# Between two layers: three projections begun early instead of two, row differences on VectorE, operands in the order of use

## The chip, the cores and the metric

The kernel runs on one core of one Trainium2 chip. The metric is the device time of one execution in microseconds (us). A core has five engines that this text names by the profile's letters: PE (TensorE, with PEld for its weight loads), DVE (VectorE), ACT (ScalarE), POOL (GpSimd) and SP (SyncE, which issues all transfers here; SPq is its DMA queue).

## The reference, cut to what matters

Two layers over x of 1024 tokens by 1024 features: a gMLP layer, then a dilated attention layer, each between two RMS norms and with a residual.

```python
for i in range(2):
    h = rms_norm(x, norm_pre[i])
    y = gmlp_mixer(h, ...) if i == 0 else dilated_attention_mixer(h, b_w_in, b_w_out, cos, sin)
    x = x + rms_norm(y, norm_post[i])

def dilated_attention_mixer(h, w_in, w_out, cos, sin):
    proj = h @ w_in                  # 1024 x 10240
    # 3 groups (window, dilation) = (128,1), (512,4), (2048,16); 16 heads of 64
    for g, (window, dilation) in enumerate(DILATED_GROUPS):
        q, k = rope(q_g), rope(k_g)
        o_g, lse_g = dilated_window_attention(q, k, v_g, window, dilation)
    alpha = softmax over g of lse_g
    return (sum_g alpha_g * o_g) * silu(z) @ w_out
```

## The kernel before, in words

**Products.** Every projection of the attention layer (layer B) is a chunk of 256 output columns for all 1024 tokens, computed as seven products instead of eight: rows and features of h are each halved (a11, a12 for tokens 0 to 511, a21, a22 for 512 to 1023), and sums and differences of the quarters are multiplied. A product is four times three matmuls of 128x128 by 128x512 (`mm3`, lines 82 to 85: each operand is split into a high and a low part), so 12 matmuls. A chunk is named by its columns: bv00, bv01, ... for values (quarter of the heads q, group g), bqk0_0_0, bqk0_0_1, ... for queries and keys (q, g, pair), bz for the gate. Below, a, b and c are the first three chunks bv00, bqk0_0_0 and bqk0_0_1, and a5 is product 5 of chunk a. Products 1 and 2 need the rows of tokens 0 to 511 alone (`put_top`), products 3 to 7 need all rows (`put_rest`): the sum a21+a22 for product 5, three differences, one after the other in place, for 7 (a11-a21), 6 (sum minus a11) and 3 (a12 minus that), and a22 for 4. `put_op` brings each of them into the operand layout: four transposes on PE (line 129, tiles pt_b), a cast on ACT (b_hi), a subtraction on DVE (b_lo). Each is done per token tile of 128, as four calls of `put_rest`, the last two (b2 and b3) for the tiles 6 and 7.

**The weights.** `Right.load` fetches four pieces of 256 KB of a chunk (lines 169 to 171, tiles wb0 to wb3), `Right.sums` forms four sums on POOL (tiles wt1, wt2, wb1, wt4), and `get` splits an operand on ACT and DVE (whi, wlo). `Right.only` fetches just the one piece that product 1 or 2 needs, and no sums. Chunk.run stores product 1 in the bank pb, 2 in pa, 5 and 3 in pc; after 2 an add on DVE reads pa, after 7 an add reads pc (for a value chunk it is `vt <- p, b_x`, line 88), and product 3 goes on in pc and must wait for that add. The banks of PSUM are three of the kind "mm", and "s", "t", "o" for the attention's own tiles (2, 2 and 1).

**The transition.** The gMLP layer's output product (`wout_unit`) ends with the tiles 6 and 7; `post` then does, for one tile after the other, the post norm (ms_pa and rstd_pa, xr), the pre norm of layer B (ms_b, rstd_b, yt) and `put_rest`. The rstd of both norms is a 128x1 power on POOL (line 106). The first four tasks of layer B (products a1, a2, b1, b2) come from `run(pipeline(tasks[:4], 3, tasks[4:]))`, and here the scheduler places instructions on PE; from the fifth task on PE goes by the order of the program (`manual_schedule`). On the other engines the scheduler sets the order throughout.

**The rest.** `drive` runs the products and, between them, steps of the attention (`step_side`: four transposes pT or more, products po, scores s of one block; lines 766 to 820), which are queued with `later`; the attention of a query and key chunk is queued when its product 3 is done, with a wait of WAIT=16 yields (a yield is three matmuls, a quarter of a product). A credit that grows by RATE=0.125 a yield, from 0.5, lets one step through at each whole: one in two products. The rotated queries and keys are stored by SP into the tiles Q and K (lines 706 and 707, 16 transfers a chunk, eight after each half).

Of the kernel before, what the change touches and what calls it, by code (L numbers as in the profile page):

```python
# [23 lines left out]
RATE = 0.125  # L24
# [10 lines left out]
def trunk_kernel(  # L35
# [97 lines left out]
        put_op(ops, 1, h0[:, 0:512], t, name)  # L133
        put_op(ops, 2, h0[:, 512:1024], t, name)

    def put_rest(pool, ops, h0, h1, t, name, first):

        a11, a12, a21, a22 = h0[:, 0:512], h0[:, 512:1024], h1[:, 0:512], h1[:, 512:1024]
        s1 = pool.tile([P, 512], F32, tag="sums", bufs=2, name=f"sums_{name}")
        add(s1, a21, a22)  # L140
        sub(a21, a11, a21, first)
        sub(a11, s1, a11, nc.gpsimd)
        sub(a12, a12, a11, nc.gpsimd)
        for i, a in ((4, a22), (5, s1), (7, a21), (6, a11), (3, a12)):
            put_op(ops, i, a, t, name)

    HALVES = (slice(0, 512), slice(512, 1024))

# [130 lines left out]
    def in_turn(chunks, early=False, banks=5):  # L279

        out, n = [], 0
        if early:
            a, b = chunks[:2]
            out = [(a, 1), (a, 2), (b, 1), (b, 2), (a, 6), (a, 5), (a, 7), (b, 6), (a, 4)]
            out += [(a, 3), (b, 5), (b, 7)] if banks == 3 else [(b, 5), (a, 3), (b, 7)]
            n = 2
        for c, last in zip(chunks[n:], [chunks[n - 1] if n else None, *chunks[n:]]):
            if banks == 3:  # L290
                out += [(c, 1), (last, 4), (last, 3), (c, 6), (c, 2), (c, 5), (c, 7)]
            else:
                out += [(c, 1), (last, 4), (c, 2), (last, 3), (c, 6), (c, 5), (c, 7)]
        out += [(chunks[-1], 4), (chunks[-1], 3)]
        return [(c, i) for c, i in out if c]
# [240 lines left out]
    with ExitStack() as octx:  # L536
# [39 lines left out]
        def post(t):  # L576
            r = rstd_of(op, sq2[t], f"pa_{t}")
            xt = op.tile([P, D], F32, tag="wk", bufs=WK, name=f"xr_{t}")
            nc.sync.dma_start(out=xt, in_=x[t * P:(t + 1) * P, :])
            for hs_ in HALVES:  # L580
                nc.vector.scalar_tensor_tensor(out=xt[:, hs_], in0=yts[t][:, hs_], scalar=r, in1=xt[:, hs_], op0=ALU.mult, op1=ALU.add)
            nc.sync.dma_start(out=x1d[t * P:(t + 1) * P, :], in_=xt)
            norm_rows(op, yts[t], xt, g1b, f"b{t}")
            hs[t] = yts[t]
            if t < 4:
                put_top(bops, hs[t], t, f"b{t}")
            else:
                put_rest(op, bops, hs[t - 4], hs[t], t - 4, f"b{t - 4}", nc.vector)

        wout_unit((0, 1, 4, 5), 0)  # L590
        wout_unit((0, 1, 4, 5), 1)
# [69 lines left out]
    def v_chunk(q, g):  # L661
        vts = {}

        def out(th, ct):
            if ct not in vts:
                vts[ct] = qk_tile(f"vt_{q}_{g}_{ct}")
            return vts[ct][:, th * 512:th * 512 + 512]

        def turned(pr):
            V = v_tile(f"V_{q}_{g}_{pr}").rearrange("p (b h d) -> p b h d", b=8, h=2)  # L670
            for b4 in range(2):
                pt = psum("t", [P, 4, P], f"pvt_{q}_{g}_{pr}_{b4}")
                for j in range(4):
                    nc.tensor.transpose(out=pt[:, j, :], in_=toks(vts[pr], g, 4 * b4 + j, 1), identity=ident)
                nc.scalar.copy(out=V[:, 4 * b4:4 * b4 + 4].rearrange("p j h d -> p j (h d)"), in_=pt)
            VS[q, g, pr] = V
            yield

        def done():
            TURN[q, g] = turned(1)  # L680
            later(turned(0), 4)

        return proj_t(wb[q * 10 + g * 3], bops, newb, f"bv{q}{g}", lambda th, ct, o: None, out=out, done=done)

    def qk_chunk(q, g, pr):
        nm = f"{q}_{g}_{pr}"
# [20 lines left out]
                nc.sync.dma_start(out=half_of(dst[o + 32:o + 64, :], g, th), in_=by_block(yc[32 * i:32 * i + 32, :], g))  # L707

        def done():
            later(lambda: attention(q, g, pr), WAIT)  # L710
            if (q, g, pr) == (3, 2, 1):
                rate[0] = RATE3

        return proj_t(wb[q * 10 + g * 3 + 1 + pr], bops, newb, f"bqk{nm}", qk_out, done=done)

    def z_chunk(q):

        def z_out(th, ct, c):
            o = newb(f"z10_{q}") if (th, ct) == (1, 0) else c
            nc.scalar.activation(out=o, in_=c, func=AF.Silu)  # L720
            if q == 3:
                SZ[q, th, ct] = o
                return
            while (q, ct, th) not in merged:
                step_slow()
            y, kept = newb(f"y_{q}_{ct}_{th}"), ybd[2 * q + ct][:, HALVES[th]]
            nc.sync.dma_start(out=y, in_=kept)
            mul(o, o, y, nc.gpsimd)
            nc.sync.dma_start(out=kept, in_=o)

        return proj_t(wb[q * 10 + 9], bops, newb, f"bz{q}", z_out, hooks={2: lambda: prep(0), 7: lambda: prep(1)} if q == 3 else None)

    merged, through = set(), set()
    slow = deque()
# [216 lines left out]
            yield  # L951

    side = deque()
    credit, rate = [0.5], [RATE]
    now = [0]

    def later(work, wait=0):
# [68 lines left out]
                chunks.append(z_chunk(q - 1))  # L1026
    chunks += [z_chunk(2), z_chunk(3)]
    tasks = in_turn(chunks, True, 3)
    run(pipeline(tasks[:4], 3, tasks[4:]))
    with tc.manual_schedule(engines={mybir.EngineType.PE}):  # L1030
        drive(pipeline(tasks[4:], 3))


    for c in (6, 7):
# [141 lines left out]
```

## Time and profile before

| | |
|---|---|
| runs | 1915.05, 1915.68, 1916.51 us, median 1915.68 us |
| profiled execution | 1915.24 us, span 1913.5 us (1.74 us lie around it) |
| mean granted clock of TensorE over the span | 0.987 of full speed |
| busy: PE, DVE, ACT, POOL | 1834.7, 1310.4, 1002.7, 503.6 us |
| DMA | 242.22 MB, mean 127 GB/s |

A row of a timeline gives the start and the duration of one instruction or of a group of equal ones (x4), and in square brackets how long the engine had idled before it and for whom. Matmuls are pipelined: one lasts 0.39 us in the rows, and the next starts 0.23 us later. PEclk is the granted clock of TensorE as a share of 2.4 GHz: 1.00 is this level, 0.50 is 1.2 GHz, and a value between is a stretch with both.

### The profile page before, as it was taken

Reading aid. Unit: us, or ns where it says so; the run is one execution under the profiler, and the core shown is the slowest. Engines: PE = TensorE matmul, PEld = TensorE weight load, DVE = VectorE, ACT = ScalarE, POOL = GpSimd, SP = SyncE. Lnnn points to the kernel's source line nnn. Section 1 sums busy time; section 2 is a strip of 40 time slices with the busy share of each in tenths; the row PEclk is TensorE's granted clock in tenths of the full one; section 3 lists DMA queues with packets and bytes.
Section 4 is the critical chain, followed back from the end, with each engine's and each line's share of the span. In section 5 each row is a group of like instructions: output and inputs, shape, how many; then the busy total and the mean of one; then the engine's idle time right before and its main releaser. Section 6 shows DMA issues by size and latency. Waiting matters only on the chain.

```text
span 1913.5 us, 29729 instructions
## 1 busy us (share of the span) xinstructions
PE 1834.7 (96%) x10024; PEld 1507.0 (79%) x10024; DVE 1310.4 (68%) x2518; ACT 1002.7 (52%) x2280; POOL 503.6 (26%) x371
## 2 busy tenths in 40 slices
PE   6899999999999997999999999999999999999998
PEld 6899888888888775777788777788777787778777
DVE  7765766577455877558587695768684876868583
ACT  6544456555544664355555557364556445555831
POOL 3431343433300204222222113321233231221320
PEclk9999999999999998999999999999999999999999
DMA  6232434433256575232233544335533336423863
GB/s 214 86 125 93 139 116 129 128 111 101 78 193 231 171 252 171 69 81 73 81 81 92 165 129 128 75 78 132 163 102 97 82 89 163 133 75 84 248 196 110
DMA packets 231847, 242.22 MB, mean 127 GB/s; under 512 B 98448, under 2 KB 150288, under 8 KB 231696
## 3 DMA queue, kind: packets, MB, share of 16 engines
q1 hardware_dynamic: 231696, 240.34, 43.5%
q8 instruction: 79, 1.29, 0.3%
q14 instruction: 72, 0.59, 0.1%
HBM read 170.46 MB, written 44.63 MB: 112 GB/s over the span
## 4 chain that ended last, share of the span: by engine, by line
PE 72%; DVE 10%; DMA 5%; issue 3%; SPq 2%; ACT 2%; POOL 1%; DVEq 0%; POOLq 0%; ACTq 0%
PE p_bqk L83 6%; PE p_bqk L84 6%; PE p_bqk L85 6%; PE p_bv L83 4%; PE p_bv L85 3%; PE p_bv L84 3%; PE s L766 3%; PE po L815 3%; PE p_z L83 3%; PE p_z L84 2%; PE p_z L85 2%; PE pT L799 2%; PE p_u L83 2%; PE p_u L84 2%; PE po L84 2%
## 5 line engine op out<-in xcount | busy, mean ns | idle before, releaser
L83 PE MATMUL p_bqk<-b_hi,whi_bqk 128*128 128x512 f32 x672 | 270.2, 402 | 1.0 <-ACT b_x_bqk L240 0.9
L84 PE MATMUL p_bqk<-b_lo,whi_bqk 128*128 128x512 f32 x672 | 263.3, 392 | 0.0
L85 PE MATMUL p_bqk<-b_hi,wlo_bqk 128*128 128x512 f32 x672 | 263.3, 392 | 0.0
L777 ACT ACTIVATE St<-St,st 128x128 f32<-128x128 f32 (+1 forms) x384 | 168.5, 440 | 153.0 <-DVE st L774 150.9
L83 PEld LDWEIGHTS p_bqk<-b_hi,whi_bqk 128*128 128x128 f32 x672 | 127.0, 189 | 41.3 <-issue 10.5
L83 PE MATMUL p_bv<-b_hi,whi_bv 128*128 128x512 f32 x336 | 137.7, 410 | 12.2 <-DVE vt L88 11.1
L85 PEld LDWEIGHTS p_bqk<-b_hi,wlo_bqk 128*128 128x128 f32 x672 | 126.8, 189 | 27.2
L84 PEld LDWEIGHTS p_bqk<-b_lo,whi_bqk 128*128 128x128 f32 x672 | 127.1, 189 | 24.4
L85 PE MATMUL p_bv<-b_hi,wlo_bv 128*128 128x512 f32 x336 | 134.4, 400 | 0.0
L84 PE MATMUL p_bv<-b_lo,whi_bv 128*128 128x512 f32 x336 | 134.0, 399 | 0.0
L774 DVE CUSTOM_DVE_ANT_0 St<-s,mask 128x128 f32<-128x128 f32 (+1 forms) x384 | 110.6, 347 | 31.5 <-PE s L766 31.5
L84 PE MATMUL p_v<-wlo_v,a_hi 128*128 128x256 f32 x448 | 127.6, 285 | 3.9 <-DVE wlo_v L91 3.9
L85 PE MATMUL p_v<-whi_v,a_lo 128*128 128x256 f32 x448 | 127.8, 286 | 3.7 <-DVE sqa L368 2.2
L83 PE MATMUL p_v<-whi_v,a_hi 128*128 128x256 f32 x448 | 127.9, 286 | 2.9 <-DVE v_s_v L88 2.2
L91 POOL TENSOR_TENSOR wt_bqk<-wb_bqk,wt_bqk 128x512 f32<-128x512 f32 x48 | 71.3, 1485 | 194.6 <-DMA wb_bqk<-in_wb_dram 147.2
L91 DVE TENSOR_TENSOR wlo_bqk<-wb_bqk,whi_bqk 128x512 fp32r<-128x512 f32 x96 | 80.8, 842 | 54.0 <-ACT whi_bqk L97 53.4
L97 ACT CAST whi_bqk<-wb_bqk 128x512 fp32r<-128x512 f32 x96 | 59.4, 619 | 107.1 <-PE p_bqk L84 70.8
L85 PE MATMUL po<-oh,yl 128*128 128x512 f32 x256 | 101.6, 403 | 3.1 <-DVE yl L91 3.1
L83 PE MATMUL po<-oh,yh 128*128 128x512 f32 x256 | 101.9, 399 | 0.6 <-ACT yh L97 0.6
L84 PE MATMUL po<-ol,yh 128*128 128x512 f32 x256 | 100.9, 397 | 1.2 <-DVE ol L91 1.2
L91 POOL TENSOR_TENSOR wt_bqk<-wb_bqk,wb_bqk 128x512 f32<-128x512 f32 x24 | 33.7, 1405 | 246.9 <-DMA wb_bqk<-in_wb_dram 172.2
L766 PE MATMUL s<-K,Q 64*128 64x128 f32 (+1 forms) x768 | 85.8, 342 | 8.5 <-DMA K<-b_c 7.5
(262 smaller groups left out, 4843.5 us busy)
## 6 DMA issues: line engine op xcount, KB each, us to landing
wb_bqk<-in_wb_dram SPq DMA_DIRECT2D x96, 256.0 KB, 3.5
wr<-in_woa_dram SPq DMA_DIRECT2D x80, 256.0 KB, 3.5
yr<-yad SPq DMA_DIRECT2D x48, 256.0 KB, 3.3
wb_bv<-in_wb_dram SPq DMA_DIRECT2D x48, 256.0 KB, 3.2
Q<-b_c SPq DMA_DIRECT2D x192, 64.0 KB, 2.1
K<-b_c SPq DMA_DIRECT2D x192, 64.0 KB, 2.1
mo<-od SPq DMA_DIRECT2D x36, 256.0 KB, 3.5
mw<-wd SPq DMA_DIRECT2D x72, 128.0 KB, 3.5
```

The lines of the kernel that those rows point to most:

```text
L83: nc.tensor.matmul(out=pso, lhsT=l_hi, rhs=r_hi, start=start, stop=False, skip_group_check=chained)
L84: nc.tensor.matmul(out=pso, lhsT=l_hi, rhs=r_lo, start=False, stop=False, skip_group_check=chained)
L85: nc.tensor.matmul(out=pso, lhsT=l_lo, rhs=r_hi, start=False, stop=stop, skip_group_check=chained)
L91: (eng or nc.vector).tensor_tensor(out=out, in0=a, in1=b, op=ALU.subtract)
L97: nc.scalar.copy(out=hi, in_=src)
L766: nc.tensor.matmul(out=pss[hh][:, cs].rearrange("p (n l) -> p n l", l=k_.shape[2]), lhsT=q_, rhs=k_, start=True, stop=True)
L774: nc.vector.tensor_tensor_reduce(out=self.S[hh][:, cs], in0=pss[hh][:, cs], in1=mk, scale=-0.125, scalar=3.0e38, op0=ALU.add, op1=ALU.min, ...
L777: nc.scalar.activation(out=self.S[hh][:, cs], in_=self.S[hh][:, cs], func=AF.Exp, scale=-1.0, bias=m, accum_out=z)
L799: nc.tensor.transpose(out=pT[hh][:, k, :], in_=self.S[hh][:, k * P:k * P + P], identity=ident)
L815: nc.tensor.matmul(out=po[64 * hh:64 * hh + 64, o:o + m * P], lhsT=V[:, kb, hh, :], rhs=self.PT[:, hh, k:k + m, :].rearrange("p k i -> p ( ...
```

## The change

`put_rest` does the second difference on DVE too (only the third stays on POOL) and calls `put_op` in the order 5, 6, 7, 4, 3. `in_turn` begins with a1 a2 b1 b2 c1 c2, and the products 3 to 7 follow. Six tasks instead of four run ahead of `drive`, in a loop of their own, in which only the six weight pieces that they need are fetched; the full loads and sums of a, b and c come with the tasks after them. The bank of product 2 of a, b and c, and pc of a, is the single "o" bank (`EARLY_TAGS`). The first attention's wait is 12 yields instead of 16, and the credit starts at 0.

```diff
-    def put_rest(pool, ops, h0, h1, t, name, first):
+    def put_rest(pool, ops, h0, h1, t, name):
...
         add(s1, a21, a22)
-        sub(a21, a11, a21, first)
-        sub(a11, s1, a11, nc.gpsimd)
+        put_op(ops, 5, s1, t, name)
+        sub(a21, a11, a21)
+        sub(a11, s1, a11)
+        for i, a in ((6, a11), (7, a21), (4, a22)):
+            put_op(ops, i, a, t, name)
         sub(a12, a12, a11, nc.gpsimd)
-        for i, a in ((4, a22), (5, s1), (7, a21), (6, a11), (3, a12)):
-            put_op(ops, i, a, t, name)
+        put_op(ops, 3, a12, t, name)
...
-            a, b = chunks[:2]
-            out = [(a, 1), (a, 2), (b, 1), (b, 2), (a, 6), (a, 5), (a, 7), (b, 6), (a, 4)]
-            out += [(a, 3), (b, 5), (b, 7)] if banks == 3 else [(b, 5), (a, 3), (b, 7)]
-            n = 2
+            a, b, c = chunks[:3]
+            out = [(d, i) for d in (a, b, c) for i in (1, 2)]
+            out += [(a, 5), (a, 6), (a, 7), (b, 6), (a, 4), (a, 3), (b, 5), (b, 7), (c, 6), (b, 4), (b, 3), (c, 5), (c, 7)]
+            n = 3
...
-            later(lambda: attention(q, g, pr), WAIT)
+            later(lambda: attention(q, g, pr), WAIT if q + g + pr else WAIT - 4)
...
+    EARLY_TAGS = {"v": ("mm", "o", "o"), "qk": ("mm", "o", "mm")}
...
-    credit, rate = [0.5], [RATE]
+    credit, rate = [0.0], [RATE]
...
-    run(pipeline(tasks[:4], 3, tasks[4:]))
+    for c, i in tasks[:4]:
+        c.early(i)
+    for n, (c, i) in enumerate(tasks[:6]):
+        run(c.run(i))
+        if n < 2:
+            tasks[n + 4][0].early(tasks[n + 4][1])
+        elif n < 4:
+            tasks[n + 4][0].prep(tasks[n + 4][1])
     with tc.manual_schedule(engines={mybir.EngineType.PE}):
-        drive(pipeline(tasks[4:], 3))
+        drive(pipeline(tasks[6:], 3))
```

PE between the layers, before (pt_b2 and pt_b3 are the transposes of the last two token tiles; the number behind is the product that the operand is for; p00 and p10 are banks):

```order
L85 MATMUL p00_bqk0_0_0_7482<-b_hi1_5163,wlo1_bqk0_0_0_7437 128x512
L129 MATMUL pt_b2_4_7287<-ident_69,yt_6_6195 128x128 x4
...
L129 MATMUL pt_b2_5_7294<-ident_69,sums_b2_7282 128x128 x4
...
L129 MATMUL pt_b2_3_7315<-ident_69,yt_2_6189 128x128 x4
L129 MATMUL pt_b3_4_7349<-ident_69,yt_7_6198 128x128 x4
...
L129 MATMUL pt_b3_3_7377<-ident_69,yt_3_6192 128x128 x4
L83 MATMUL p00_bv00_7444<-b_hi6_5173,whi6_bv00_7459 128x512
```

and with the change:

```order
L85 MATMUL p00_bqk0_0_0_7464<-b_hi1_5163,wlo1_bqk0_0_0_7413 128x512
L129 MATMUL pt_b2_5_7284<-ident_69,sums_b2_7282 128x128 x4
L83 MATMUL p00_bqk0_0_1_7519<-b_hi1_5163,whi1_bqk0_0_1_7439 128x512
...
L129 MATMUL pt_b2_3_7315<-ident_69,yt_2_6189 128x128 x4
...
L85 MATMUL p00_bqk0_0_1_7519<-b_hi1_5163,wlo1_bqk0_0_1_7440 128x512
L129 MATMUL pt_b3_5_7346<-ident_69,sums_b3_7344 128x128 x4
...
L129 MATMUL pt_b3_3_7377<-ident_69,yt_3_6192 128x128 x4
L83 MATMUL p10_bqk0_0_0_7498<-b_hi2_5165,whi2_bqk0_0_0_7418 128x512
```

All of b1 now stands ahead of the last two tiles' transposes; c1 stands among those of tile b2, three matmuls behind pt_b2_5, three behind pt_b2_7 and six behind pt_b2_3; b2 and then c2 stand behind the last transpose, pt_b3_3.

POOL between the layers, before (rstd_pa and rstd_b are the two norms of the tiles 6 and 7, yt_2 and yt_3 the differences of the last two `put_rest` calls, the rest are weight sums):

```order
L91 TENSOR_TENSOR wt4_bv00_7408<-wb2_bv00_7400,wt2_bv00_7407 128x512
L106 TENSOR_TENSOR rstd_pa_6_7263<-ms_pa_6_7260,nhalf_74 128x1
L91 TENSOR_TENSOR wt1_bqk0_0_0_7429<-wb1_bqk0_0_0_7425,wb0_bqk0_0_0_7421 128x512
L106 TENSOR_TENSOR rstd_b6_7278<-ms_b6_7275,nhalf_74 128x1
...
L106 TENSOR_TENSOR rstd_b7_7340<-ms_b7_7337,nhalf_74 128x1
L91 TENSOR_TENSOR wt2_bqk0_0_0_7430<-wb3_bqk0_0_0_7427,wt1_bqk0_0_0_7429 128x512
L91 TENSOR_TENSOR yt_3_6192<-sums_b3_7344,yt_3_6192 128x512
L91 TENSOR_TENSOR yt_3_6192<-yt_3_6192 128x512
```

and with the change:

```order
L106 TENSOR_TENSOR rstd_pa_6_7263<-ms_pa_6_7260,nhalf_74 128x1
L91 TENSOR_TENSOR wt1_bv00_7487<-wb1_bv00_7483,wb0_bv00_7479 128x512
L106 TENSOR_TENSOR rstd_b6_7278<-ms_b6_7275,nhalf_74 128x1
...
L91 TENSOR_TENSOR wt4_bv00_7489<-wb2_bv00_7481,wt2_bv00_7488 128x512
L91 TENSOR_TENSOR yt_2_6189<-yt_2_6189 128x512
L91 TENSOR_TENSOR wt1_bqk0_0_0_7565<-wb1_bqk0_0_0_7561,wb0_bqk0_0_0_7557 128x512
L106 TENSOR_TENSOR rstd_b7_7340<-ms_b7_7337,nhalf_74 128x1
L91 TENSOR_TENSOR wt2_bqk0_0_0_7566<-wb3_bqk0_0_0_7563,wt1_bqk0_0_0_7565 128x512
L91 TENSOR_TENSOR wb1_bqk0_0_0_7561<-wb3_bqk0_0_0_7563,wb1_bqk0_0_0_7561 128x512
L91 TENSOR_TENSOR yt_3_6192<-yt_3_6192 128x512
```

The sums of bv00 stood ahead of rstd_pa_6 and now stand behind it, among the norms; two sums of bqk0_0_0 now stand between rstd_b7 and the last difference, where one stood.

PE at the chunk bv11, some 350 us later, before (p00_bv11 holds product 4, p20_bv11 product 3, s_1_0_0_3 are the scores of a step of the attention):

```order
L85 MATMUL p00_bv11_10247<-b_hi4_5169,wlo4_bv11_10484 128x512
L799 MATMUL pT_1_0_0_2_0_10609<-ident_69,St_1_0_0_2_0_10559 128x128 x4
...
L815 MATMUL po_1_0_0_1_10621<-PT_1_0_0_1_10532,V_1_0_0_9961 64x128 x2
L766 MATMUL s_1_0_0_3_0_10631<-K_1_0_0_10073,Q_1_0_0_10072 128x256
L766 MATMUL s_1_0_0_3_1_10632<-K_1_0_0_10073,Q_1_0_0_10072 128x256
L83 MATMUL p20_bv11_10487<-b_hi3_5167,whi3_bv11_10516 128x512
```

and with the change:

```order
L804 MATMUL pT_1_0_0_2_0_10603<-ident_69,St_1_0_0_2_0_10555 128x128 x4
...
L771 MATMUL s_1_0_0_3_1_10626<-K_1_0_0_10090,Q_1_0_0_10089 128x256
L83 MATMUL p00_bv11_10309<-b_hi4_5169,whi4_bv11_10511 128x512
...
L85 MATMUL p00_bv11_10309<-b_hi4_5169,wlo4_bv11_10512 128x512
L887 MATMUL wT_0_1_10660<-ident_69,e_0_1_10493 48x128
L83 MATMUL p20_bv11_10515<-b_hi3_5167,whi3_bv11_10565 128x512
```

The step that stood between the products 4 and 3 of bv11 now stands ahead of product 4. The steps of the attention have moved by one product in this way, from behind every second product to behind the others.

## Rows read from the trace of the kernel before

**Rows 1.** The page, busy time of PE (us, share of the span, instructions)

```profile
PE 1834.7 (96%) x10024; PEld 1507.0 (79%) x10024; DVE 1310.4 (68%) x2518; ACT 1002.7 (52%) x2280; POOL 503.6 (26%) x371
```

**Rows 2.** The page, the chain that ended last, shares of the span

```profile
PE 72%; DVE 10%; DMA 5%; issue 3%; SPq 2%; ACT 2%; POOL 1%; DVEq 0%; POOLq 0%; ACTq 0%
```

**Rows 3.** Windows between the layers: window, length, busy time per engine, PEclk, DMA share, GB/s

```profile
740.00:745.00 5.00, 1.74 (x8) 1.12 (x6) 3.39 (x10) 1.96 (x5) 2.28 (x3) 0.99 0.43 166
...
745.00:770.00 25.00, 19.35 (x66) 14.97 (x67) 15.78 (x26) 8.95 (x18) 9.72 (x7) 0.59 0.27 91
```

**Rows 4.** Timeline of PE between the layers

```profile
745.85 1.09 PE L129 MATMUL pt_b<-ident,yt 128*128 128x128 f32 x4 [4.11 <-DVE yt L155]
...
755.77 1.09 PE L129 MATMUL pt_b<-ident,yt 128*128 128x128 f32 x4 [3.10 <-DVE yt L155]
...
762.65 0.80 PE L83 MATMUL p_bv<-b_hi,whi_bv 128*128 128x512 f32 x1 [1.16 <-ACT b_s_bv L240]
...
768.37 0.58 PE L84 MATMUL p_bqk<-b_lo,whi_bqk 128*128 128x512 f32 x1
768.78 0.40 PE L85 MATMUL p_bqk<-b_hi,wlo_bqk 128*128 128x512 f32 x1
```

**Rows 5.** Timeline of POOL between the layers

```profile
739.15 0.55 POOL L106 TENSOR_TENSOR rstd_pa<-ms_pa,nhalf 128x1 f32<-128x1 f32 x1
...
743.71 0.55 POOL L106 TENSOR_TENSOR rstd_b<-ms_b,nhalf 128x1 f32<-128x1 f32 x1
...
746.90 2.47 POOL L91 TENSOR_TENSOR wb_bqk<-wb_bqk,wb_bqk 128x512 f32<-128x512 f32 x1 [2.13 <-DMA wb_bqk<-in_wb_dram]
...
757.70 1.28 POOL L91 TENSOR_TENSOR yt<-sums_b,yt 128x512 f32<-128x512 f32 x1 [3.55 <-DVE yt L91]
759.05 1.27 POOL L91 TENSOR_TENSOR yt<-yt 128x512 f32<-128x512 f32 x1
```

**Rows 6.** Timeline of DVE between the layers

```profile
736.78 0.14 DVE L104 TENSOR_SCALAR ms_pa<-ms_pa 128x1 f32<-128x1 f32 x1
...
747.55 0.68 DVE L91 TENSOR_TENSOR yt<-yt,yt 128x512 f32<-128x512 f32 x1
```

**Rows 7.** Waits of PE from 770 us on: us in total, times, longest

```profile
PE p_bv L83 <- DVE vt L88: 11.1, 4, 3.2
PE s L766 <- DMA K<-b_c: 7.5, 10, 1.4
```

**Rows 8.** Timeline of PE at bv02 and bv11

```profile
930.24 0.50 PE L83 MATMUL p_bv<-b_hi,whi_bv 128*128 128x512 f32 x1 [1.89 <-DVE vt L88]
...
1088.35 0.50 PE L83 MATMUL p_bv<-b_hi,whi_bv 128*128 128x512 f32 x1 [3.18 <-DVE vt L88]
```

**Rows 9.** Windows around stalls of PE (columns as in rows 3)

```profile
930.00:936.00 6.00, 5.76 (x26) 4.70 (x27) 1.48 (x3) 1.44 (x6) 0.00 (x0) 1.00 0.12 11
1088.00:1095.00 7.00, 6.65 (x23) 5.20 (x24) 1.58 (x3) 1.65 (x6) 1.28 (x1) 0.76 0.40 106
...
1500.00:1510.00 10.00, 8.17 (x46) 6.25 (x46) 8.89 (x23) 4.70 (x18) 5.19 (x3) 0.83 0.47 113
```

**Rows 10.** Timeline of PE where scores wait for K

```profile
810.70 0.46 PE L766 MATMUL s<-K,Q 64*128 64x128 f32 x2 [0.49 <-DMA K<-b_c]
811.81 0.89 PE L766 MATMUL s<-K,Q 64*128 64x128 f32 x6 [0.65 <-DMA K<-b_c]
...
1503.56 0.46 PE L766 MATMUL s<-K,Q 64*128 64x128 f32 x2 [0.99 <-DMA K<-b_c]
1504.86 1.13 PE L766 MATMUL s<-K,Q 64*128 64x128 f32 x14 [0.84 <-DMA K<-b_c]
...
1670.06 0.89 PE L766 MATMUL s<-K,Q 64*128 64x128 f32 x6 [1.44 <-DMA K<-b_c]
```

**Rows 11.** Timeline of SP's queue at the first attention

```profile
798.57 0.61 SPq L706 DMA_DIRECT2D Q<-b_c  x1
...
809.69 0.59 SPq L707 DMA_DIRECT2D K<-b_c  x1
```

More of the change, by code (lines that the diff above doesn't have):

```diff
@@ L587, in post @@
             else:
-                put_rest(op, bops, hs[t - 4], hs[t], t - 4, f"b{t - 4}", nc.vector)
+                put_rest(op, bops, hs[t - 4], hs[t], t - 4, f"b{t - 4}")
         wout_unit((0, 1, 4, 5), 0)
@@ L681, in done @@
             later(turned(0), 4)
-        return proj_t(wb[q * 10 + g * 3], bops, newb, f"bv{q}{g}", lambda th, ct, o: None, out=out, done=done)
+        return proj_t(wb[q * 10 + g * 3], bops, newb, f"bv{q}{g}", lambda th, ct, o: None, EARLY_TAGS["v"] if q == g == 0 else ("mm",) * 3, out=out, done=done)
     def qk_chunk(q, g, pr):
@@ L709, in done @@
         def done():
-            later(lambda: attention(q, g, pr), WAIT)
+            later(lambda: attention(q, g, pr), WAIT if q + g + pr else WAIT - 4)
             if (q, g, pr) == (3, 2, 1):
                 rate[0] = RATE3
-        return proj_t(wb[q * 10 + g * 3 + 1 + pr], bops, newb, f"bqk{nm}", qk_out, done=done)
+        return proj_t(wb[q * 10 + g * 3 + 1 + pr], bops, newb, f"bqk{nm}", qk_out, EARLY_TAGS["qk"] if q == g == 0 else ("mm",) * 3, done=done)
     def z_chunk(q):
```

## The prediction

> **What bounds the kernel now.** The page comes first: PE is busy for 96% of the span [rows 1] and makes 72% of the chain that ended last [rows 2]. Nothing gets faster here unless PE idles less or keeps its higher clock for longer. So I looked for PE's idle time in two places that the edit touches. The first is the stretch between the layers. By windows PE is busy for 1.74 of the 5 us from 740, and from 745 to 770 its mean granted clock is 0.59 [rows 3]. The timeline says why: three waits for the norms of the last two tiles, 4.11, 3.10 and 1.16 us, and then half clock (matmuls 0.43 us apart) until about 768.6 [rows 4]. The second is the long phase after 770. Its list of waits has two large entries, 11.1 us for the add `vt` and 7.5 us for the keys' transfers [rows 7]. The change moves the steps of the attention by one product, so it reaches both.
>
> **The change, part by part, gains positive.**
>
> *Between the layers.* POOL did the four weight sums of bv00 ahead of rstd_pa of tile 6, which started at 739.15 [rows 5], though DVE had its input ready at 736.9 [rows 6]. The sums now stand behind. I put rstd_pa at 737.6, a shift of 1.5 us. rstd_b of tile 6 (743.71 before [rows 5]) has one weight sum ahead of it as before, and the tile's first transpose moves from 745.85 [rows 4] to about 744.8; it is now that of the sum, which DVE has 0.7 us after yt. All of b1 stands before it, six matmuls more, so PE stops at about 742.9 and waits some 1.9 us instead of 4.11. Then comes c1, 12 matmuls, the only new filler: b2 and c2 still stand behind the last transpose. After c1 PE has nothing until tile 7's norm. That one gains little. rstd_b of tile 7 waits on POOL behind a sum of bqk0_0_0, whose pieces are loaded later than before. I put its yt 1.3 us earlier, and PE's wait at 4.2 us where 3.10 stood. The second difference costs 0.68 us on DVE, by the difference it does already, instead of 1.28 on POOL [rows 5, 6]. But two sums of some 1.26 us each now stand between tile 7's norm and the last difference, where one stood. The last transpose therefore ends about when it did, and dense work starts at about 762.6 again (bounds 761 and 764.5).
>
> From there on 12 matmuls fewer are left, 12 x 0.23 = 2.7 us. Against that stand new waits from one bank to the next: c2 waits for the add that reads b2's bank, a5 for the one on c2, and a7 for the ACT copy of a6. The nearest row is the 1.16 us that PE waited for an ACT copy [rows 4], the shortest possible is the 0.68 of such a DVE operation [rows 6]. I take 0.9 each, together 2.7. Net 0. For the bounds: if the clock stays down for the 24 matmuls of b2 and c2 instead of the first 14 to 15 [rows 4], it is 2 us worse, and a start at 764.5 costs 2 more: -4. With the waits hidden and a start at 761 it is +4.
>
> A rule of the Trainium skill bears on the moved difference: "SBUF — State Buffer", "Who interferes with whom", says that a DVE instruction with two inputs in SBUF and a GpSimd one that reads SBUF exclude each other for the whole instruction. The 2.47 us of a POOL sum beside DVE's `yt<-yt,yt`, against 1.28 without [rows 5, 6], fits it. By that rule each moved difference could push a POOL sum by 0.68 us, and the sum of this part would be about -1 instead of 0, inside its bounds.
>
> *Waits for vt.* Product 3 of a value chunk goes on in the bank that the add `vt` still has to read. Where a step of the attention stands between the products 4 and 3, that add stands on DVE behind the step's four masked scores, and PE waits: 1.89 us at bv02, 3.18 at bv11 [rows 8], 3.0 at bv21 and at bv31, 11.1 in all [rows 7]. By the order, with the change the step stands ahead of product 4 at bv02, bv11, bv21 and bv31, and DVE has the 12 matmuls of product 4 to catch up. At bv01, bv10, bv20, bv30 and bv32 a step now stands between 4 and 3. At the middle three DVE does the add ahead of the step's scores, as it did before at bv12 and bv22, which do not wait. Two are left, bv01 and bv32. Their price lies between 1.89 and 3.18 each, and I take 2.2, near the lower, since both stand in an early group like bv02. Gain 11.1 - 4.4 = 6.7 (bounds 4.7 and 11.1).
>
> *Clock.* After each of the three 3 us stalls the clock falls: 0.76 over 7 us [rows 9], so 0.24 x 7 = 1.7 us lost, three times. The 1.89 us stall cost none (1.00 [rows 9]). These 5.0 us come back. One such loss is new, at the first attention (next paragraph), -1.7. Gain 3.3; bounds 0, if both remaining stalls and one for keys lose the clock too, and 5.
>
> *Keys.* The first step of an attention waits for K. Before the first one, SP issues 16 transfers from 798.57 to 809.69 [rows 11], and PE, with four products (48 matmuls, 10.9 us) to do after bqk0_0_0 is finished, waits 0.49 + 0.65 = 1.1 us [rows 10]. Now it has three products, 8.2 us, 2.7 less, with one weight load fewer in SP's burst (0.6 us): 3.1 to 4.5 us, taken 3.8. Elsewhere the lead is four products and a few small matmuls, 51 to 54 matmuls, and rows of this kind show 1.44 at 54 and 0.99 + 0.84 at 51 [rows 10]. Before the change the order has six attentions with such a lead; with it nine: six of 53 to 54 matmuls (taken 0.9 each: the 7.5 us [rows 7], less 1.1 for the first and 3.3 for two at 51 matmuls and their like, leave 3.1 over four, 0.8) and three of 52 (1.45 each). That is 3.8 + 5.5 + 4.4 = 13.7 against 8.2 (7.5 and 0.7 put down to issue in the same steps): -5.5, bounds -11 (1.8 at all nine) and -2 (the shortest at all).
>
> *The rest.* The final product and the last steps lie as before; 0, cover: the same products follow in the same order. If the shift leaves a last step uncovered, a step is worth about 1 us.
>
> **Sum**: 0 + 6.7 + 3.3 - 5.5 = +4.5 us. The profiled execution took 1915.24, so 1910.7 by that account; the median of the runs lies 0.4 above it, so I give **1911.1 us**. About 0.2%, 3.8 us, is what a measurement of this kernel can tell from no change.
>
> **The rivals.**
> 1. *The filler works in full.* c1 removes its 2.7 us, the earlier norms 1.5, and the clock stays up as PE idles less. For: POOL's sums really were in the way [rows 5]. Against: tile 7's chain hangs on weight pieces loaded later. It gives 4 to 5 us on top: 1906.
> 2. *The transition turns late.* Either the last difference or the clock comes later, -4 in this part: 1915, no change. For: c2 and a5 wait on one bank right where the clock should rise. Half clock held for 14 to 15 matmuls after 762.65 though PE hardly paused [rows 4]. The Trainium skill, "TensorE: Matmul & The Clock Gate", "A second HAM failure mode: psum-queue depth-cycling", warns of just this: short idles between groups that cycle through PSUM banks keep throwing the clock back. The 0.76 windows agree that a wait is paid twice; that 1.89 us cost none speaks for the sum above.
> 3. *Slower: the keys decide.* Every lead of four products waits 1.8 us, as at 1504 [rows 10], and three of them lose the clock as there (0.83 over 10 us [rows 9], 1.7 us). Then the keys cost -11 and -5 of clock: 0 + 6.7 + 3.3 - 11 - 5 = -6, 1921. It decides from about 1.3 us a lead upward with the clock lost at two. Against: 1.44 at a lead of 54 is already the longest single wait of its kind [rows 7, 10].
> 4. *The stalls only move.* If the adds at bv10, bv20 and bv30 do wait, the vt part gives about 0 and the clock -1.7: 0 - 1.7 - 5.5 = -7, 1922. Against: bv12 and bv22.
> 5. *The edit doesn't do what it says*: b2 and c2 stand behind the last transpose, so there are not three early products to fill with. That is already in the sum.
>
> **How the numbers follow.** Forecast 0.42 (two thirds of it beyond 0.2%, the bounds reaching 1907 to 1915), rival 1 0.20 (faster), rival 2 0.17 (mostly within 0.2%), rivals 3 and 4 together 0.21 (slower for 0.12; half-way forms of them end within 0.2%, or a little faster). So faster 0.51, same 0.33, slower 0.16. The range takes in rival 1 with its bound and half of rivals 3 and 4: 1903.5 to 1919.
>
> **What would show it.** Right: the waits for vt after 770 fall to 4 to 5 us, two of them, at bv01 and bv32; the windows of 0.76 at bv11, bv21 and bv31 are gone; the waits for K rise to 13 or 14 us with one of 3 to 4.5 at the first attention; between the layers dense work starts at about 762.6 after a PE wait of some 4 us for tile 7. Wrong: vt waits of about 3 us at bv10, bv20 and bv30; K waits that stay at 8 or pass 18; dense work that starts before 760 or after 765, or a clock that has not risen by 772.

## The result, and the profile after

| | before | changed |
|---|---|---|
| median of 5 runs | 1915.68 us | 1925.13 us |
| lowest and highest | 1915.05, 1917.38 | 1924.32, 1932.14 |
| profiled execution, span | 1915.24, 1913.5 | 1929.51, 1927.8 |

The ratio is 1.0063 (95% interval 1.0051 to 1.0075): slower, where a gain of 0.2% was forecast. The profiled execution is one of the longer of its five, so sizes from it are rather high; a second one of the same kernel (e12 below) stands beside it where that matters.

The page of the changed kernel, busy time of each engine, which answers to [rows 1]: PE is busy 3 us longer at the same work, and idle for 11 more.

```profile
PE 1837.7 (95%) x10024; PEld 1508.6 (78%) x10024; DVE 1313.8 (68%) x2522; ACT 999.0 (52%) x2278; POOL 504.3 (26%) x367
```

Between the layers, the timeline of PE after the change (it answers to [rows 4]):

```profile
745.28 0.63 PE L129 MATMUL pt_b<-ident,sums_b 128*128 128x128 f32 x4 [2.87 <-DVE sums_b L88]
...
748.64 1.09 PE L129 MATMUL pt_b<-ident,yt 128*128 128x128 f32 x4 [1.82 <-DVE yt L91]
...
759.99 1.08 PE L129 MATMUL pt_b<-ident,sums_b 128*128 128x128 f32 x4 [5.23 <-DVE sums_b L88]
...
764.93 0.66 PE L129 MATMUL pt_b<-ident,yt 128*128 128x128 f32 x4 [1.36 <-POOL yt L91]
767.59 0.80 PE L83 MATMUL p_bqk<-b_hi,whi_bqk 128*128 128x512 f32 x1 [2.00 <-DVE vt L88]
...
773.93 0.50 PE L83 MATMUL p_bqk<-b_hi,whi_bqk 128*128 128x512 f32 x1 [0.85 <-DVE b_s_bqk L88]
...
777.80 0.50 PE L83 MATMUL p_bv<-b_hi,whi_bv 128*128 128x512 f32 x1 [0.85 <-DVE b_s_bqk L88]
...
784.55 0.50 PE L83 MATMUL p_bv<-b_hi,whi_bv 128*128 128x512 f32 x1 [1.01 <-ACT b_x_bv L242]
```

The three waits at 773.93, 777.80 and 784.55 are the ones forecast from bank to bank (c2, a5, a7), at 0.85 to 1.01 us each. The wait of 5.23 us for tile 7's norm is 1 us longer than forecast and ends 5 us later. The 2.00 us at 767.59 was not forecast at all: b2 needs the o bank of a2, and the add that empties it stands on DVE behind all the operands of the last tile (it runs at 766.86, although a2 was through at 739.7). Dense products start at 767.59 instead of 762.65.

Why the norm is late stands in the timelines of DVE and POOL. First DVE in the kernel before, `xr` of tile 7 and the sum of squares ms_b of its norm:

```profile
746.89 0.74 DVE L581 SCALAR_TENSOR_TENSOR xr<-yt,rstd_pa,xr 128x512 f32<-128x512 f32 x1
...
748.75 0.63 DVE L88 TENSOR_TENSOR ms_b<-sqn_b 128x1 f32<-128x1 f32 x1
```

Then DVE and POOL in the changed kernel (they answer to [rows 6] and [rows 5]); the `xr` at 745.05 is that of tile 7:

```profile
743.37 1.76 DVE L88 TENSOR_TENSOR sums_b<-yt 128x512 f32<-128x512 f32 x1
745.05 1.76 DVE L583 SCALAR_TENSOR_TENSOR xr<-yt,rstd_pa,xr 128x512 f32<-128x512 f32 x1
746.74 1.75 DVE L91 TENSOR_TENSOR yt<-yt,yt 128x512 f32<-128x512 f32 x1
...
754.63 0.15 DVE L88 TENSOR_TENSOR ms_b<-sqn_b 128x1 f32<-128x1 f32 x1
...
757.70 1.42 DVE L157 SCALAR_TENSOR_TENSOR yt<-xr,rstd_b,g1b 128x512 f32<-128x512 f32 x2 [1.66 <-POOL rstd_b L106]
```

```profile
743.18 1.41 POOL L91 TENSOR_TENSOR wt_bv<-wb_bv,wt_bv 128x512 f32<-128x512 f32 x1 [1.32 <-DMA wb_bv<-in_wb_dram]
744.55 1.72 POOL L91 TENSOR_TENSOR wb_bv<-wb_bv,wb_bv 128x512 f32<-128x512 f32 x1
746.23 1.71 POOL L91 TENSOR_TENSOR wt_bv<-wb_bv,wt_bv 128x512 f32<-128x512 f32 x1
...
755.51 1.65 POOL L91 TENSOR_TENSOR wt_bqk<-wb_bqk,wb_bqk 128x512 f32<-128x512 f32 x1 [4.39 <-DVE ms_b L104]
757.12 0.54 POOL L106 TENSOR_TENSOR rstd_b<-ms_b,nhalf 128x1 f32<-128x1 f32 x1
```

From 743 to 748 POOL does the weight sums of bv00, which the change moved out of the way of rstd_pa and into the middle of the norms. Each of the three DVE instructions beside them takes 1.75 us where 0.68 to 0.75 is usual, and the sums take up to 1.7 us where 1.3 is usual. That costs DVE 3.2 us, but tile 7's `xr` still ends at 746.8, no later than before (747.6). What comes late is the next step. ms_b of tile 7 stands on DVE behind the operands of tile 6 and starts at 754.63, 7.8 us after that `xr`; in the kernel before it was 1.1 us. Then rstd_b waits on POOL behind one more sum, of bqk0_0_0. How much of this is the order on DVE and how much the sums is a question for e2, e3, e5 and e8.

After 770, the list of PE's waits in the changed kernel (it answers to [rows 7]):

```profile
PE s L771 <- DMA K<-b_c: 7.8, 7, 3.0
PE pT L804 <- ACT St L782: 7.1, 10, 1.5
PE bpo L83 <- ACT yl L97: 4.4, 1, 4.4
PE p_bv L83 <- DVE vt L88: 4.2, 3, 2.2
PE wT L887 <- DVE e L94: 4.0, 1, 4.0
PE s L771 <- issue: 3.3, 4, 1.4
PE pT L804 <- ACT wTs L889: 2.5, 2, 1.4
```

The same list of the kernel before, the entries that [rows 7] leaves out:

```profile
PE pT L799 <- ACT St L777: 3.1, 7, 0.9
PE wT L882 <- DVE e L94: 2.6, 1, 2.6
PE bpo L85 <- POOL yl L91: 2.1, 2, 1.7
PE bpo L83 <- ACT yl L97: 1.0, 1, 1.0
...
PE s L766 <- issue: 0.7, 1, 0.7
```

The waits for vt fell from 11.1 to 4.2 us, as forecast. The transposes' waits for ACT rose from 3.1 to 9.6 us, and at the end the output product waits 4.39 us for ACT (`bpo`), where it waited 1.0. The first attention waits 3.02 us for K, and behind it the clock is down: 0.83 in the mean over 20 us, where the kernel before has 1.00.

```profile
821.85 0.76 PE L771 MATMUL s<-K,Q 64*128 64x128 f32 x2 [3.02 <-DMA K<-b_c]
823.14 1.61 PE L771 MATMUL s<-K,Q 64*128 64x128 f32 x6 [0.53 <-DMA K<-b_c]
```

```profile
808.00:828.00 20.00, 16.45 (x63) 12.39 (x62) 13.46 (x25) 6.81 (x16) 5.61 (x4) 0.83 0.36 98
```

and the same window of the kernel before:

```profile
808.00:828.00 20.00, 18.86 (x95) 14.80 (x94) 14.71 (x34) 11.40 (x29) 5.71 (x4) 1.00 0.36 97
```

### The profile page after: what moved, and what is told of

Same layout as the page of the kernel before. It is cut to its first block, busy times and chain, and to the rows that moved or that the text cites. A ratio compares the mean times of both kernels' runs of the same rounds, so it can differ in the third digit from the quotient of the medians.

```text
span 1927.8 us, 29732 instructions
## 1 busy us (share of the span) xinstructions
PE 1837.7 (95%) x10024; PEld 1508.6 (78%) x10024; DVE 1313.8 (68%) x2522; ACT 999.0 (52%) x2278; POOL 504.3 (26%) x367
## 5 line engine op out<-in xcount | busy, mean ns | idle before, releaser
L91 DVE TENSOR_TENSOR wlo_bqk<-wb_bqk,whi_bqk 128x512 fp32r<-128x512 f32 x92 | 81.0, 881 | 46.7 <-ACT whi_bqk L97 42.9
```

Source lines behind the costliest of these rows:

```text
L91: (eng or nc.vector).tensor_tensor(out=out, in0=a, in1=b, op=ALU.subtract)
```

## The experiments

Each run was compared with the kernel before on the same chip, where that took 1914.5 to 1915.6 us in the median of 11 to 22 runs and spread from 1908 to 1922. Single runs say little at this spread, so I also measured stretches in the profiles, from the start of the last product row of the gMLP layer (PE, line 85, `po`) on. The columns: start of the dense products; the first 72 matmuls of layer B done (the 73rd starts); start of the 29th product, behind the first attention's first steps and bv01; from there to the 263rd product, near the end of the projections (the long phase); from there to the last matmul. At the 29th and the 263rd product every kernel has the same matmuls of the attention behind it.

| profile | dense | 72 done | 29th | long phase | end |
|---|---|---|---|---|---|
| before | 28.2 | 39.3 | 111.8 | 896.3 | 163.6 |
| changed | 33.8 | 44.0 | 125.4 | 891.7 | 169.7 |
| e12 changed, again | 33.1 | 43.0 | 123.8 | 891.9 | 169.3 |
| e1 steps shifted alone | 27.7 | 37.6 | 110.5 | 885.6 | 168.1 |
| e2 put_rest alone | 31.0 | 39.3 | 111.9 | 894.6 | 161.0 |
| e3 changed, old put_rest | 30.7 | 40.9 | 122.2 | 894.7 | 167.3 |
| e4 changed, old steps | 34.0 | 43.8 | 125.5 | 892.7 | 163.7 |
| e5 changed, no sums | 25.9 | 36.1 | 117.5 | 895.0 | 169.4 |
| e6 changed, longer lead | 32.7 | 42.9 | 118.4 | 891.4 | 169.0 |
| e7 changed, other banks | 30.8 | 36.7 | 117.4 | 889.7 | 168.8 |
| e8 both | 30.3 | 36.4 | 111.8 | 891.6 | 168.5 |
| e9 e8, steps back at the end | 32.0 | 37.6 | 113.0 | 891.6 | 163.0 |
| e10 e9, first sums early | 29.6 | 35.1 | 110.6 | 887.3 | 165.3 |
| e11 e1, steps back at the end | 28.2 | 38.4 | 111.3 | 888.5 | 164.9 |

Read by columns: the changed kernel loses 12 to 14 us up to the 29th product and 6 in the end, and gains some 4 in between. The stretches scatter as well. The kernel before, e1 and e11 are one program up to the 72nd matmul and differ by 1.7 us there; the two profiles of the changed kernel differ by 1.6 us at the 29th product. The long phase lies between 885.6 and 895.0 us with shifted steps (mean 891) and between 892.7 and 896.3 with the old ones (mean 894.5), so a single pair does not show its gain.

**e1, the shift of the steps alone.**

```diff
-    credit, rate = [0.5], [RATE]
+    credit, rate = [0.0], [RATE]
```

> The kernel before with one edit: the credit of the attention's steps starts at 0 instead of 0.5, so that every step moves by one product, as in the change; nothing else. Theory A (the change loses its time between the layers and at the first attention, which has three products of lead; the shift of the steps by itself is worth little, since it gives back some 5 us in the long phase and takes some 6 us at the end): 1915 to 1918 us, waits for vt down to 4 to 5 us with one of some 2 us at bv01, a longer end (the last wT waits 4 us instead of 2.6). The first attention has five products of lead here and shows no wait for K. Theory B (the shift itself is what costs, by waits of transposes for ACT and of scores for K): 1920 us or more. Theory C (the shift is the good part, as forecast): 1909 to 1912 us.

Measured: 1919.0 us in the median of six, from 1909.0 to 1921.5; ratio 1.0016 (0.9992 to 1.0040), no difference shown. The profiled run was the fastest of the six, and four of the six took 1917 us or more, so its stretches show the shift at its best. They have the forecast signs: the long phase 10.7 us shorter, the end 4.5 longer. The whole times alone do not rule out theory B, whose 1920 us lies inside the interval; but nothing of the 12 us up to the 29th product is here, so the shift is not what costs them. Between A and C this run does not decide.

**e2, put_rest alone**: its part of the diff in the kernel before.

> The kernel before with one edit: the new put_rest (second difference on DVE, operands in the order 5, 6, 7, 4, 3); two early chunks, steps and weights as before. Theory A (what delays the dense products is that the norm of the last tile stands on DVE behind the operands of the tile before it, an order that came with the new put_rest): dense products start 3 to 5 us later than at 762.65 and the run takes 1918 to 1921 us. Theory D (the weight sums of POOL, which now run beside the norms and hold up DVE, are what delays them; the new put_rest alone is harmless or a gain): 1913 to 1916 us, dense products at 761 to 763.

Measured: 1912.4 us, ratio 0.9989 (0.9969 to 1.0010), no difference shown. ms_b of tile 7 stands behind the operands of tile 6 here too, 21.5 us after the last product row (14.3 in the kernel before, 20.8 in the changed one), with the sums of bqk0_0_0, and none of bv00, among the norms on POOL. Dense products start 2.8 us later than in the kernel before, but the 72 matmuls are through at the same 39.3: their matmuls follow at 0.23 us from the second on, where the kernel before has 14 at 0.43. Theory A's mechanism is there, at half its size, and costs nothing in the sum.

**e3, the changed kernel with the old put_rest.**

> The changed kernel with the put_rest of before (second difference on POOL, operands 4, 5, 7, 6, 3), three early chunks and their weights as in the change. Theory A: dense products start 3 to 5 us earlier than at 767.6, the run takes 1920 to 1922 us. Theory D: the start stays at 767 or comes later, since POOL has one more difference to do among the sums: 1925 to 1928 us.

Measured: 1926.3 us, ratio 1.0067 (1.0046 to 1.0088), the time of the changed kernel. With the old order ms_b of tile 7 comes 15.4 us after the last product row instead of 20.8, and dense products start some 3 us earlier, although DVE's instructions beside the sums still last 1.75 to 1.78 us. The loss in time stays. Timeline of DVE in e3:

```profile
747.26 1.78 DVE L88 TENSOR_TENSOR sums_b<-yt 128x512 f32<-128x512 f32 x1
748.97 1.76 DVE L581 SCALAR_TENSOR_TENSOR xr<-yt,rstd_pa,xr 128x512 f32<-128x512 f32 x1
750.66 1.75 DVE L91 TENSOR_TENSOR yt<-yt,yt 128x512 f32<-128x512 f32 x1
```

So neither with the old put_rest nor with the old steps (e4) is the loss gone.

**e4, the changed kernel with the steps of before.** Two things differ here: the first attention's wait is also cut to 8 yields, which leaves it two products of lead.

```diff
-    credit, rate = [0.0], [RATE]
+    credit, rate = [0.5], [RATE]
...
-            later(lambda: attention(q, g, pr), WAIT if q + g + pr else WAIT - 4)
+            later(lambda: attention(q, g, pr), WAIT if q + g + pr else 8)
```

> The changed kernel with the credit started at 0.5 (the steps fall as in the kernel before) and the first attention's wait at 8 yields, which leaves it two products of lead instead of three. Theory A: the first attention waits 2.7 us longer for K (6 us in all), the long phase loses its 5 us (three waits of 3 us for vt with half clock behind them are back), the end wins 6: 1925 to 1929 us. Theory B (the shift costs): 1918 to 1921 us.

Measured: 1927.2 us, ratio 1.0070 (1.0052 to 1.0089), inside theory A's span. The wait for K is 6.0 us, 3 more than at three products of lead, and the waits for vt are back, 10.8 us in four waits:

```profile
823.91 0.76 PE L771 MATMUL s<-K,Q 64*128 64x128 f32 x2 [6.01 <-DMA K<-b_c]
...
1102.72 0.79 PE L83 MATMUL p_bv<-b_hi,whi_bv 128*128 128x512 f32 x1 [2.98 <-DVE vt L88]
```

The end is at 163.7, the value of the kernel before.

**e5, without the sums** of the first three chunks on POOL (other operands stand in, so these columns are not the product asked for).

```diff
+            if self.name in ("bv00", "bqk0_0_0", "bqk0_0_1"):
+                self.raws = {1: b11, 6: b12, 2: b21, 7: b12, 5: b11, 4: b21, 3: b22}
+                return
```

> The changed kernel without the four weight sums of POOL for the first three chunks (their operands stand in for them, so that these columns are not the product asked for). Theory D (the sums now run beside the last norms: they hold DVE's two-input operations up, 1.76 us instead of 0.69 three times, and one stands ahead of the last norm on POOL): the DVE operations are back at 0.7 us, dense products start at 761 to 763 instead of 767.6, the run takes 1917 to 1921 us. Theory E (the order on DVE, where the last tile's norm stands behind the operands of the tile before, sets the start): start at 765 or later, 1922 to 1925 us.

Measured: dense products start 25.9 us after the last product of the layer before instead of 33.8, and the 72 matmuls are through 7.8 us earlier. The DVE instructions are back at their usual length (timeline of DVE in e5):

```profile
742.30 0.69 DVE L88 TENSOR_TENSOR sums_b<-yt 128x512 f32<-128x512 f32 x1
742.91 0.75 DVE L586 SCALAR_TENSOR_TENSOR xr<-yt,rstd_pa,xr 128x512 f32<-128x512 f32 x1
743.57 0.69 DVE L91 TENSOR_TENSOR yt<-yt,yt 128x512 f32<-128x512 f32 x1
```

Dense products start earlier still than theory D had it (759.6), and E, by which the start would stay at 765 or later, falls: ms_b still stands behind tile 6's operands, but comes 15.2 us after the row. The edit takes the sums away altogether, so it prices their place in POOL's queue and their effect on DVE together and does not tell them apart. The run's time, 1923.2 us (ratio 1.0042, 1.0026 to 1.0057), is above what D gave and inside what E gave, and its interval overlaps that of the changed kernel, so no gain in time is shown. In its profile 4.8 of the 7.8 us are left at the last matmul, and the long phase is 3 us longer, which no edit explains.

**e6, a product more of lead for the first attention.**

```diff
-(b, 5), (b, 7), (c, 6), (b, 4), (b, 3), (c, 5), (c, 7)]
+(b, 5), (b, 7), (b, 4), (b, 3), (c, 6), (c, 5), (c, 7)]
```

> The changed kernel with products 4 and 3 of the second chunk one place earlier (a5 a6 a7 b6 a4 a3 b5 b7 b4 b3 c6 c5 c7), so that the first attention has four products of lead instead of three; the step itself stays where it is. If the short lead costs its wait and the half clock behind it (3.55 us of waiting against 1.1 before, and 10 us at a clock of 0.66): the wait falls to some 1 us and the run by 4 to 6 us, to 1919 to 1921. If the wait only moves to another place: 1923 to 1926.

Measured: 1922.0 us, ratio 1.0041 (1.0026 to 1.0056). The wait for K is 0.30 us, the clock of the same 20 us is 1.00 (0.83 in the changed kernel), and from the 72nd matmul to the 29th product it takes 75.6 us instead of 81.5 and, in e12, 80.8. The median fell by 3 us, less than the 4 to 6 expected. The window of e6:

```profile
808.00:828.00 20.00, 19.70 (x95) 15.46 (x94) 15.52 (x36) 10.50 (x27) 5.64 (x4) 1.00 0.41 112
```

**e7, other banks for the products 2.**

```diff
-    EARLY_TAGS = {"v": ("mm", "o", "o"), "qk": ("mm", "o", "mm")}
+    EARLY_TAGS = {"v": ("mm", "o", "o"), "qk0": ("mm", "s", "mm"), "qk1": ("mm", "t", "mm")}
```

> The changed kernel with product 2 of the second and third chunk in a bank of the kinds s and t, which are free once the transposes are through, instead of the single o bank. If the shared bank costs its waits (2.00 us behind the add on a2, 0.85 behind b2, 0.85 behind c2): these three rows are gone and the run takes 3 to 4 us less, 1921 to 1922. If they hide behind the clock or the next wait: no change, 1924 to 1926.

Measured: 1921.6 us, ratio 1.0035 (1.0023 to 1.0047). The three waits of 2.00, 0.85 and 0.85 are gone, and the 72 matmuls are through 6.3 to 7.3 us earlier than in the two profiles of the changed kernel. Waits make 3.7 us of it and the clock 2.3: the twelve matmuls of b2 take 5.5 us in the changed kernel, 0.43 apart to the last, and 3.2 in e7, where they stand 0.23 apart from the fourth on. The rest is the start of the last transposes, which differs from profile to profile. The timeline of PE in e7:

```profile
767.98 0.40 PE L83 MATMUL p_bqk<-b_hi,whi_bqk 128*128 128x512 f32 x1
768.21 0.39 PE L84 MATMUL p_bqk<-b_lo,whi_bqk 128*128 128x512 f32 x1
```

**e8, both of these edits.**

> Both of these edits together. If the two costs are separate they add up: 1915 to 1918 us, about the kernel before. If they share one wait: 1919 to 1922.

Measured: 1915.3 us, ratio 1.0006 (0.9993 to 1.0018). At the 29th product the two costs nearly add up, 7.0 and 8.0 us apart and 13.6 together, and with them gone the changed kernel is level with the kernel before; the 29th product starts at the same 111.8.

This profile also settles what the longer DVE instructions cost. Here POOL's sum gives way and lasts 3.69 us, and the same three DVE instructions keep their usual length (timelines of POOL and DVE in e8):

```profile
739.37 3.69 POOL L91 TENSOR_TENSOR wt_bv<-wb_bv,wt_bv 128x512 f32<-128x512 f32 x1 [2.12 <-DMA wb_bqk<-in_wb_dram]
```

```profile
738.76 0.68 DVE L88 TENSOR_TENSOR sums_b<-yt 128x512 f32<-128x512 f32 x1
739.36 0.74 DVE L583 SCALAR_TENSOR_TENSOR xr<-yt,rstd_pa,xr 128x512 f32<-128x512 f32 x1
740.02 0.68 DVE L91 TENSOR_TENSOR yt<-yt,yt 128x512 f32<-128x512 f32 x1
...
748.77 0.15 DVE L88 TENSOR_TENSOR ms_b<-sqn_b 128x1 f32<-128x1 f32 x1
```

Yet ms_b of tile 7 comes 19.4 us after the last product row, where e7, with the same banks and two of the three DVE instructions at 1.75 us or more, has 19.9, and dense products start 0.5 us earlier than there. In both kernels the third difference of tile 6, which stands on POOL behind the sums, starts 16 us after the row (11.9 in e5). So the late norm does not hang on the length of the DVE instructions; it comes from the new order on DVE together with the sums among the norms, whichever engine gives way. With the old order (e3), or with no sum there (e5, e10), ms_b comes 3 to 6 us earlier.

**e9, the steps back in their old place at the end.**

```diff
+            if (q, g, pr) == (3, 1, 0):
+                credit[0] += 0.5
```

> The changed kernel with the two edits of e8_lead_banks, and with half a credit added once, when the chunk bqk3_1_0 is done: from there on the steps fall again as in the kernel before. If the shift of the steps costs its 6 us only in the last two hundred us (the last key wait with half clock, and the output product's wait of 4 to 6 us for ACT), while the long phase keeps its gain: 5 to 7 us less than e8_lead_banks, 1908 to 1911 us, and a wait of bpo for ACT back at 1 to 2 us. If the end's cost has another cause: 1913 to 1917.

Measured: 1909.9 us, ratio 0.9974 (0.9962 to 0.9985), below the kernel before, and 5.4 below e8, which ran on another chip (by the ratios 6). The wait of `bpo` for ACT is 0.73 us. The row that goes with it is on ACT: the last copy oT of the attention waits for its buffer, which a store to memory still reads, and ACT holds the output product's operand behind it. ACT in the changed kernel, then in e9:

```profile
1815.09 0.59 ACT L825 COPY oT<-po 128x512 f32<-128x512 f32 x1 [5.16 <-DMA od<-oT]
```

```profile
1798.85 0.59 ACT L827 COPY oT<-po 128x512 f32<-128x512 f32 x1 [1.79 <-DMA od<-oT]
```

**e10, the first chunk's sums ahead of the norms again**, on top of e9.

```diff
-    for c, i in tasks[:4]:
-        c.early(i)
+    for c, i in tasks[:2]:
+        c.prep(i)
+    for c, i in tasks[2:4]:
+        c.early(i)
```

> As e9_tail, with the first chunk loaded in full and its sums done on POOL ahead of the last norms, as in the kernel before; the other two early chunks fetch their single pieces. If the sums beside the norms are what makes the dense products start late: they start 2 to 5 us earlier counted from the last output product of the layer before (30 us after it in e8_lead_banks), and the run takes 2 to 4 us less than e9_tail. If the loads of the full chunk hold up the first products or the first norm by as much: no gain over e9_tail, or up to 3 us lost.

Measured: 1908.6 us, ratio 0.9963 (0.9948 to 0.9978). DVE's instructions are at 0.68 to 0.75 us, dense products start at 29.6 and the 72 matmuls are through at 35.1, 2.5 us before e9. The medians of e9 and e10 differ by 1.3 us, and their intervals overlap: the gain between the layers is there, a gain in time over e9 is not shown.

**e11, the kernel before with the steps shifted, and shifted back at the end.**

> The kernel before with the steps shifted (credit from 0, as in e1_phase_alone) and shifted back when bqk3_1_0 is done; nothing between the layers is changed. If the shift gains 5 us or more in the long phase and costs 6 at the end: 1908 to 1911 us where the kernel before takes 1915. If the long phase gains nothing by it: 1914 to 1917.

Measured: 1908.9 us, ratio 0.9965 (0.9953 to 0.9977). With nothing changed between the layers this is as fast as e10.

**e12, the changed kernel again**, beside e9 to e11.

> The changed kernel itself once more, beside the others on the same chip, so that its stretches can be compared within one chip: 1924 to 1930 us; dense products 33 to 34 us after the last output product of the layer before.

Measured: 1925.3 us, ratio 1.0049 (1.0031 to 1.0067), dense products at 33.1.

## Why the prediction was wrong

What failed is the "net 0" between the layers, the gain put down to the clock, and two terms put at nothing, the transposes and the end. By terms, in the profiled executions (losses positive; the clock's loss is worked out as the missing share of the granted clock in windows of 10 us, summed over those below 0.97 from 780 us to the end of the dense work). The medians differ by 9.5 us and not by the 15 of this pair, so its terms are rather high:

| term | forecast | measured | from |
|---|---|---|---|
| between the layers, with the wait of a7 | 0 | +5.3 | 44.0 - 39.3, and 0.6 to the 13th product |
| waits for vt | -6.7 | -6.9 | 4.2 against 11.1 |
| waits for keys | +5.5 | +2.9 | 7.8 + 3.3 against 8.2 |
| clock | -3.3 | +5 | 13 against 8 |
| transposes waiting for ACT | 0 | +6.5 | 7.1 + 2.5 against 3.1 |
| end (bpo, wT) | 0 | +2.7 | 8.4 against 5.7 |

The sum of the measured column, 15.5, closes on the 15.0 us by which the two profiles differ from the last gMLP product to the last matmul.

- **"Net 0" between the layers failed**, first in the step "dense work starts at about 762.6 again". The sum put tile 7's `yt` 1.3 us earlier; it came 3.5 us later (757.70 in place of 754.23). Two things were left out. The new put_rest puts ms_b of tile 7 on DVE behind tile 6's operands; the prediction had its norm wait behind POOL's sums alone. With the old put_rest it comes 14.2 to 15.4 us after the last product row, whether the sums of bv00 stand beside it (e3) or not, and with the new one 19.4 to 21.5, but 15.2 and 16.5 where no sum stands on POOL ahead of tile 6's third difference (e5, e10). And I charged the sums that left rstd_pa's way only their place in POOL's queue. That they and DVE's instructions with two operands in SBUF hold each other up was in sight in the 2.47 us of one sum [rows 5]. The Trainium skill's rule, "SBUF — State Buffer", "Who interferes with whom", is that such a DVE instruction and a GpSimd one that reads SBUF exclude each other. I applied it to the moved difference alone, which gave -1, and not to the sums as a whole; the runs agree with it, with 1.75 us on DVE beside the sums (e3) and 0.69 without them (e5), or 3.69 us on POOL (e8). e5 puts the sums at 6.9 to 7.8 us up to the 72nd matmul, but in no whole time is that price shown.
- **The waits from bank to bank** were forecast right where each follows directly (0.85, 0.85, 1.01 against 0.9 each). What I missed is the first of the chain, 2.00 us: the add on a2's bank stands on DVE behind the last tile's operands. e7 takes it away, and with it the half clock of b2. These waits alone undo the net 0: e8 has the late norm as well, yet without them it is through the 72 matmuls at 36.4, 2.9 us ahead of the kernel before. So rival 2, the late transition, was the nearest to what came, in both its parts, though the 1915 us it gave were not. The Trainium skill's rule that it named ("TensorE: Matmul & The Clock Gate", "A second HAM failure mode: psum-queue depth-cycling") is that short idles between groups that cycle through PSUM banks make the clock go back and forth. The runs bear out only a part of it: behind the 2.00 us wait the clock rose after 12 matmuls of b2, and without it after three; it did not fall again, for behind the two waits of 0.85 us after 773.93 matmuls follow at 0.23.
- **The first attention**: the wait was right (3.55 us in two pieces, 3.8 forecast; 6.0 in e4 and 0.3 in e6 fit a price of 2.7 us a product). The half clock behind it was priced at 1.7 us and was 3.4 (0.17 of 20 us); e12 shows 1.8 in the same window. e6 gets both back. The nine later leads were priced too high: 7.5 us together where the sum had 9.9.
- **The waits for vt** fell as forecast, at bv01 (2.15) and bv32 (1.89), with none at bv10, bv20 and bv30, and the half clock at bv11, bv21 and bv31 went with them. The gain did not stay whole: PE now waits 9.6 us at the transposes, where it had waited 3.1. That term is missing from the sum; what the shifted scores stand behind on DVE and ACT was not asked.
- **The end was put at 0** "since the same products follow in the same order". They do, but the attention's last steps come one product later, and the ACT copy of the last one waits for a store with the output product's operand behind it. e9 against e8 and e11 against e1 show it: 161 to 165 us with the old steps there, 167 to 170 with the shifted ones, and some 5 us in the time from e8 to e9. The clock falls there too, and that is most of its term: from 1780 to 1850 us it is 0.90 in the changed kernel (0.93 in e12) and 0.98 in the kernel before. The price of "about 1 us" for an uncovered step rested on no row. That the copy's wait for the store is the cause is argued from the rows, for no run takes that wait away by itself.
- Rivals 3 and 4 (keys, stalls that move) forecast the slower time for reasons that the runs do not show: the later leads waited 0.8 us in the mean and not 1.8, and the three adds in question did not wait. That 1925 us lies near their 1921 and 1922 is chance.

So the shift is the good part of this change as long as it is taken back at the end, and the three early chunks are the bad one. e11 keeps the shift alone, mended at the end, and wins 0.35%; without that mending no gain is shown (e1). The three early chunks, with their banks and the first attention's lead as they stand, cost 8 to 11 us (ratios 1.0049 and 1.0063 against 1.0006 in e8), and nothing once these two are mended. Beyond that they gain some 3 us up to the 72nd matmul (e10 against e11: 35.1 and 38.4), of which 0.7, within the scatter, is left at the 29th product; no gain in time is shown.

## What to carry to other kernels

When work is moved out of the way of a critical instruction, ask what it lands beside and what now stands behind it, on every engine: here DVE's instructions went from 0.7 to 1.75 us beside POOL's sums, or a sum from 1.3 to 3.7 us, and the norm was late either way. Before products share a bank, look up where the instruction that empties it stands on its engine. Filler put ahead of a wait earns only what the chain behind the wait does not hand back; here its results sat in one bank and its price was the next attention's lead. A shift of side work against the main products can be good in one stretch and bad in another, so price it by stretches, the last one too, and shift it back where it turns.

## What was not expected of the hardware

The program up to the last gMLP product is the same in its arithmetic in all these kernels, yet in the fourteen profiles that product's last row starts between 729.4 and 738.2 us. Little of the change lies ahead of it (weight loads and sums of the first chunks), and that is not the cause: seven profiles whose programs differ only behind it (the changed kernel, e4, e6 to e9, e12) lie between 729.4 and 736.1. Whole runs of one kernel spread further (the kernel before: 1908 to 1922 on one chip). It is why stretches counted from that row tell kernels apart that single times do not. The clock's answer to a stall also varies from run to run: after a wait for K of 3.0 us the granted clock over the same 20 us was 0.83 in one execution of the changed kernel and 0.91 in the other.
